# One decoder layer on one core: weight and activation tiles at other byte offsets in SBUF, and two of the three products of a K step in the other order

## The chip, the core and the metric

The kernel runs on one core of a Trainium2 chip. The metric is the device time of one execution in microseconds. The engines are named as in the profile: PE is TensorE's matmul, PEld its weight load, DVE is VectorE, ACT is ScalarE, POOL is GpSimd and SP is SyncE, whose queue issues most of the DMAs.

## The reference

One layer of a decoder in float32, for 256 tokens behind 16 meta tokens (T = 272), width 2048:

```python
q, c_kv, q_idx, k_idx, w_idx, u = split_columns(h @ w_in[l])
...
attn_out = jnp.einsum('bthc,chd->bthd', o_lat, w_uv[l]).reshape(B, T, ATTN_WIDTH)
pool_out = multiscale_pool(u, w_pool[l], pool_scale[l])
mix = jnp.concatenate([attn_out, pool_out], axis=-1) @ w_o[l]
h = layer_norm(ALPHA * h + mix, ln1_g[l], ln1_b[l])
f = conv_gated_ffn(h, w_up[l], conv_w[l], conv_b[l], w_down[l])
h = layer_norm(ALPHA * h + f, ln2_g[l], ln2_b[l])
```

`conv_gated_ffn` is a product of 2048 by 2 x 5632 columns, a causal convolution of width 3, a gated GELU and a product of 5632 by 2048. Almost all arithmetic is in four products: the input projection, `w_o`, `w_up` and `w_down`. The attention between them keeps the 64 best keys of each query.

## The kernel before

All weights come in tiles of 128 x 2048 float32, 1 MB each, in one fixed stream: 8 tiles of index queries, two small latent maps, 16 more projection tiles, 16 of `w_o`, then for the feed-forward part 88 tiles of `w_up` interleaved with the tiles of `w_down`. A tile is fetched by SP into `wraw`, and then split into an upper part, which ACT writes (L149, a copy rounded to the type that TensorE reads as fp32r), and a lower part, the remainder, which DVE writes (L150). Both go into one buffer `whl`; there are three of these and three of `wraw`. Activations are split in the same way into upper and lower parts, which lie together in one slot of a ring of 24.

`product` (L250 to L260) multiplies a weight tile with 16 activation slots, one K step of 128 for each. A K step is three matmuls into the same PSUM tile: upper weight x upper activation (L258), upper weight x lower activation (L259), lower weight x upper activation (L260). The weight block of 128 x 128 is the stationary operand, loaded by PEld for each matmul; the activation, 256 to 272 columns, streams. So one tile is 16 x 3 = 48 matmuls. The activations are named `xp` (the input, in the projection), `mixa` and `mixp` (attention and pooling, under `w_o`), `fold` (slots of another pool, for the first 8 tiles of `w_up`) and `hp` (the other 80 tiles of `w_up`). In `seven` (L855 to L857) and at L907 to L909 and L1061 to L1063, the products with `w_down`, the weights stream, 512 columns at a time, and a block of gated activations is stationary.

What matters here is where in a partition these operands begin, in bytes modulo 256. The pools are laid out by their sizes:

- A ring slot before has 2 x 272 floats, 2176 bytes, which is 8.5 times 256: neighbouring slots are 128 apart modulo 256. Inside a slot the class `Parts` puts the upper part of `mixa`, `mixp` and `hp` at 24 bytes and the lower part at 1120.
- A weight buffer before has 4160 floats, 65 times 256 bytes, so all three begin at the same place. The class `Split` puts the upper and the lower part of the first eight K steps at 0 and 4096 bytes, and those of the last eight at 8320 and 12416, which is 128 further modulo 256. The upper and the lower block of one K step are thus always at the same place. A `gap` tile of 64 bytes stands behind the buffers and shifts the ring by 64.
- The tables `K_PROJ`, `K_O` and `K_UP` say which K step stands at which place of a tile, so that slots of one kind meet the first half and slots of the other kind the second half.

Taken together, in the 80 tiles with `hp` the upper part of an activation always lies 216 bytes (modulo 256) behind the weight block that it meets, and the lower part 32 bytes behind it. Under `w_o` consecutive steps change between the two halves, since they are taken in another order (`order`).

The order of instructions on each engine comes from the program's order and a scheduler's rules; the PE queue runs in order.

Of the kernel before, what the change touches and what calls it, by code (L numbers as in the profile page):

```python
# [11 lines left out]
F32 = mybir.dt.float32  # L12
F32R = mybir.dt.float32r
# [4 lines left out]
P = 128  # L18
# [3 lines left out]
T = NM + S  # L22
Q0 = NM - 2
NQ = T - Q0
KT = D // P
# [42 lines left out]
class Split:  # L68

    def __init__(self, tile, sums):

        self.tile, self.places = tile, ((0, 1040), (2080, 3120)) if sums else ((0, 1024), (2080, 3104))

    def __getitem__(self, key):
        rows, part, c = key
        a, b = c.start, 2 * 1024 + 2 if c.stop is None else c.stop
        at = int(a >= 1024)
        assert b <= 1024 or at == 1  # L80
        o = self.places[at][part] - 1024 * at
        return self.tile[rows, o + a:o + b]


class Parts:


    def __init__(self, slot):
        flat = slot.rearrange("p a b -> p (a b)")
        self.parts = flat[:, 6:6 + NQ], flat[:, 280:280 + NQ]  # L90

    def __getitem__(self, key):
        return self.parts[key[1]][key[0], key[2]]

K_PROJ = (1, 3, 5, 7, 9, 11, 13, 15, 0, 2, 4, 6, 8, 10, 12, 14)
K_O = (1, 3, 5, 7, 9, 10, 12, 14, 0, 2, 4, 6, 8, 11, 13, 15)
K_UP = (1, 3, 5, 7, 8, 10, 12, 15, 0, 2, 4, 6, 9, 11, 13, 14)  # L100
# [3 lines left out]
def tile_layer(ctx, tc, xt, w_first, w_proj, w_uk, w_uv, w_pool, w_o, w_up, w_down, cols, rows, rel_bias, onehot, out):  # L104
    nc = tc.nc
    sb = ctx.enter_context(tc.tile_pool(name="sb", bufs=1))
    wp = ctx.enter_context(tc.tile_pool(name="wp", bufs=3))
    ring = ctx.enter_context(tc.tile_pool(name="ring", bufs=24))
# [12 lines left out]
    ps = small()  # L121
# [4 lines left out]
    stream = [w_proj[j] for j in range(8)] + [w_uk, w_uv] + [w_proj[j] for j in range(8, 24)]  # L126
    stream += [w_o[j] for j in range(KT)]
    plan = ffn_plan()
    kinds = {}
    for item in plan:  # L130
        if item[0] == "up":
            stream.append(w_up[item[2] * FT + item[1]])
        elif item[0] == "down":
            n = PARTS[FAST]
            stream.append(w_down[sum(PARTS[:FAST]) + n // 2 + (item[2] - 1) // 2 * (n // 4) + item[3]])
        else:
            kinds[len(stream)] = item[0]
            stream.append(w_down[sum(PARTS[:item[1]]) + item[2] * (PARTS[item[1]] // 2) + item[3]])
    stream += [w_down[d] for d in range(FT - PARTS[-1], FT)]
    spare, last = len(stream) - PARTS[-1], len(stream) - 1  # L140
# [29 lines left out]
            parts = split_part(raw, hl, slice(a, b))  # L170
        return parts

    def split_tile(sums=False):

        hl = Split(wp.tile([P, 4160], F32R, tag="whl", name="whl"), sums)
        if not state["use"]:

            wp.tile([P, 16], F32, tag="gap", name="gap", bufs=1)
        return hl

    def weight_tiles(sums=False):
        raw = wp.tile([P, 2048], F32, tag="wraw", name="wraw")
        return raw, split_tile(sums)

    def emit(i):
        if i in ready:
            return
        if i == last:

            raw = wp.tile([P, 2048], F32, tag="wraw", name="wraw")  # L190
            nc.sync.dma_start(raw, stream[i])
            raws[i] = raw
            ready[i] = []
            for c in range(0, 2048, 256):
                hl = ring.tile([P, 2, 258], F32R, tag="act", name="whl_r", padded_shape=[P, 2, T])
                nc.scalar.activation(hl[:, 0, :256], raw[:, c:c + 256], AF.Copy)
                nc.vector.tensor_tensor(hl[:, 1, :256], raw[:, c:c + 256], hl[:, 0, :256].bitcast(F32), op=ALU.subtract)
                ready[i].append(hl)
            return
        if i == spare:  # L200
            raw = wp.tile([P, 2048], F32, tag="wraw", name="wraw")
            hl = Split(sb.tile([P, 4160], F32R, tag="y", name="whl_y"), True)
        else:
            raw, hl = weight_tiles(i > spare)
        ready[i] = hl
        if i == VALUES:

            nc.sync.dma_start(raw, stream[i])
            held.extend((raw, hl))
            return  # L210
        split[i] = fetch(raw, hl, stream[i], kinds.get(i), i and i - 1 in split and split[i - 1][1])
        if i >= spare:
            raws[i] = raw
# [37 lines left out]
    def product(ps, hl, act, lo, hi, places, ks=None, k0=0, k1=KT):  # L251

        for n in range(k0, k1):
            k = (places if ks is None else ks)[n]
            w = slice(P * places.index(k), P * places.index(k) + P)
            wh, wl = hl[:, 0, w], hl[:, 1, w]
            ah, al = act[k][:, 0, lo:hi], act[k][:, 1, lo:hi]
            nc.tensor.matmul(ps, wh, ah, start=n == 0, stop=False)  # L258
            nc.tensor.matmul(ps, wh, al, start=False, stop=False)  # L259
            nc.tensor.matmul(ps, wl, ah, start=False, stop=n == KT - 1)  # L260

    at = ctx.enter_context(ExitStack())
    ap_ = at.enter_context(tc.tile_pool(name="attn", bufs=1))
# [3 lines left out]
    for k0, k1 in [(k, k + 1) for k in range(9)] + [(9, 12), (12, 15), (15, 16)]:  # L267
        if k0 == KT - 1:

            raw = ap_.tile([P, 1024], F32, name="wraw_l", tag="v1")[:, :T + MF].rearrange("p (a b) -> p a b", a=1)  # L270
        elif k0 % 3 == 0:
            raw = wp.tile([P, 2048], F32, tag="wraw", name="wraw")
            raw = raw[:, :3 * (T + MF)].rearrange("p (a b) -> p a b", b=T + MF)
        if k0 % 6 == 0:
            hl = split_tile()
        for w in ((slice(0, T), slice(T, T + MF)) if k0 == 0 else (slice(0, T + MF),)):
            nc.sync.dma_start(raw[:, k0 % 3:k0 % 3 + k1 - k0, w], w_first[k0:k1, :, w].rearrange("k p c -> p k c"))
        for k in range(k0, k1):
            xk, wk, a0 = raw[:, k % 3, :T], raw[:, k % 3, T:], k % 6 // 3 * 1024 + k % 3 * MF
            c = slice(a0, a0 + MF)  # L280
            a = ring.tile([P, 2, T], F32R, tag="act", name="xp")
            nc.scalar.activation(a[:, 0, :], xk, AF.Copy)
            nc.scalar.activation(hl[:, 0, c], wk, AF.Copy)
            nc.vector.tensor_tensor(a[:, 1, :], xk, a[:, 0, :].bitcast(F32), op=ALU.subtract)
            nc.vector.tensor_tensor(hl[:, 1, c], wk, hl[:, 0, c].bitcast(F32), op=ALU.subtract)
            x_parts.append(a)
            first.append((hl, c.start))
# [76 lines left out]
    ps = small()  # L364
# [225 lines left out]
    def values(h, pts, ptx):  # L590
        ps = small()
        hs = slice(h * HD, (h + 1) * HD)
        nc.tensor.matmul(ps[:, :NQ], vs[0][:, hs], ptx, start=True, stop=False)
        nc.tensor.matmul(ps[:, 2:NQ], vs[1][:, hs], pts[:, :2 * P], start=False, stop=False)
        nc.tensor.matmul(ps[:, 2 + P:NQ], vs[2][:, hs], pts[:, 2 * P:], start=False, stop=True)
        a = Parts(ring.tile([P, 2, T], F32R, tag="act", name="mixa"))
        nc.scalar.activation(a[:, 0, :NQ], ps[:, :NQ], AF.Copy)
        nc.vector.tensor_tensor(a[:, 1, :NQ], ps[:, :NQ], a[:, 0, :NQ].bitcast(F32), op=ALU.subtract)
        mix[h] = a
# [33 lines left out]
    def pooled(g, df, hl):  # L633
        for j in range(2):
            ps = small()
            for c in range(2):
                w = slice(256 * c + j * P, 256 * c + j * P + P)
                nc.tensor.matmul(ps[:, :NQ], hl[:, 0, w], df[:, c, 0, :], start=c == 0, stop=False)
                nc.tensor.matmul(ps[:, :NQ], hl[:, 0, w], df[:, c, 1, :], start=False, stop=False)
                nc.tensor.matmul(ps[:, :NQ], hl[:, 1, w], df[:, c, 0, :], start=False, stop=c == 1)  # L640
            m = 2 * g + j
            a = Parts(ring.tile([P, 2, T], F32R, tag="act", name="mixp"))
# [126 lines left out]
    def normalise(m):  # L769
        yd = y[:, m, Q0:]  # L770
        nc.vector.tensor_tensor(yd, yd, rs, op=ALU.mult)  # L771
        nc.vector.tensor_tensor(yd, yd, m2, op=ALU.add)
        nc.scalar.activation(yd, yd, AF.Identity, bias=col(LN1, 2 * m + 1), scale=col(LN1, 2 * m))
        a = Parts(ring.tile([P, 2, T], F32R, tag="act", name="hp"))
        nc.scalar.activation(a[:, 0, :NQ], yd, AF.Copy)
        nc.vector.tensor_tensor(a[:, 1, :NQ], yd, a[:, 0, :NQ].bitcast(F32), op=ALU.subtract)  # L776
        h_parts.append(a)
# [45 lines left out]
    def forms(r, j, whole):  # L823
# [9 lines left out]
        right = ring.tile([P, 2, T], F32R, tag="act", name="right")  # L833
# [321 lines left out]
```

## Time and profile before

| | |
|---|---|
| timed executions | 1034.94 us median of 2 (1034.75 to 1035.13) |
| span of the profiled execution | 1032.8 us, 2.1 us less than the median |
| PE busy | 1025.7 us, 7644 matmuls |
| PEld busy | 977.2 us, 7644 weight loads |
| DVE, ACT, POOL busy | 890.4, 622.4, 187.0 us |
| granted clock of TensorE | 0.997 of 2.4 GHz over the span |

The span runs from the first to the last instruction; what the timed executions have above it lies around the span. A PE row's duration overlaps the next matmul's, and its end is modelled. What a matmul costs in a stream is the time from its start to the start of the next, so the timeline's starts are what is read here, over as many matmuls as possible, since a start is printed to 0.01 us.

### The profile page before, as it was taken

What the parts mean: (1) busy time and instruction counts of PE and PEld (TensorE: products, weight loads), DVE (VectorE), ACT (ScalarE), POOL (GpSimd) and SP (SyncE); (2) the same over time, 40 slices, a digit from 0 to 9 for tenths busy, and PEclk for the clock granted to TensorE, in tenths of its full rate; (3) what the DMA queues carried; (4) which work ended last, traced back from release to release, by engine and by line L of the source; (5) the groups of instructions that cost most, each with busy time, mean ns of one, the idle gap of its engine ahead of it and who ended that gap; (6) DMA issues with size and microseconds to landing.
All of it is one profiled execution on the core that took longest, in us unless ns stands there. A gap on an engine that the chain in (4) does not pass through costs nothing.

```text
span 1032.8 us, 19199 instructions
## 1 busy us (share of the span) xinstructions
PE 1025.7 (99%) x7644; PEld 977.2 (95%) x7644; DVE 890.4 (86%) x1401; ACT 622.4 (60%) x1000; POOL 187.0 (18%) x245
## 2 busy tenths in 40 slices
PE   9999999999999999999999999999999999999997
PEld 8999999999999999999999999999999999999986
DVE  6878668758779998889999999999998999998976
ACT  7666446645448865655665555656556565565675
POOL 1200014125430022111121111211112111120031
PEclk9999999999999999999999999999999999999998
DMA  9755643454553569979887788877988878887875
GB/s 329 258 179 203 242 146 116 149 184 162 188 204 124 204 204 251 270 284 306 274 281 272 271 298 279 276 274 275 290 279 279 274 286 281 277 276 268 298 229 155
DMA packets 59754, 250.28 MB, mean 242 GB/s; under 512 B 21734, under 2 KB 22416, under 8 KB 32656
## 3 DMA queue, kind: packets, MB, share of 16 engines
q1 hardware_dynamic: 34592, 230.42, 61.7%
q0 software_dynamic: 7888, 16.14, 8.3%
q10 hardware_dynamic: 17184, 2.49, 1.5%
q8 instruction: 60, 0.98, 0.4%
q14 instruction: 30, 0.25, 0.1%
HBM read 232.50 MB, written 2.11 MB: 227 GB/s over the span
## 4 chain that ended last, share of the span: by engine, by line
PE 91%; DVE 4%; issue 2%; ACT 1%; POOL 1%; DMA 0%; SPq 0%; POOLq 0%; DVEq 0%; ACTq 0%
PE mm L260 22%; PE mm L258 22%; PE mm L259 22%; PE at L857 6%; PE at L856 6%; PE at L855 6%; PE mm L331 2%; DVE whl L150 1%; PE mm L909 1%; PE mm L908 1%; PE mm L907 1%; ACT whl L149 1%; DVE x L771 0%; DMA wraw<-in_w_first 0%; PE mm L559 0%
## 5 line engine op out<-in xcount | busy, mean ns | idle before, releaser
L150 DVE TENSOR_TENSOR whl<-wraw,whl 128x1024 fp32r<-128x1024 f32 (+1 forms) x416 | 486.8, 1205 | 35.7 <-ACT whl L149 34.7
L149 ACT ACTIVATE whl<-wraw 128x1024 fp32r<-128x1024 f32 (+1 forms) x416 | 403.1, 1015 | 108.1 <-DMA wraw<-in_w_up 21.4
L260 PE MATMUL mm<-hp,whl 128*128 128x258 f32 x1280 | 362.8, 283 | 0.0
L258 PE MATMUL mm<-hp,whl 128*128 128x258 f32 x1280 | 359.5, 281 | 0.0
L259 PE MATMUL mm<-hp,whl 128*128 128x258 f32 x1280 | 357.2, 279 | 0.3 <-DVE hp L776 0.3
L258 PEld LDWEIGHTS mm<-hp,whl 128*128 128x128 f32 x1280 | 243.8, 190 | 3.2
L259 PEld LDWEIGHTS mm<-hp,whl 128*128 128x128 f32 x1280 | 240.4, 188 | 3.7 <-DVE hp L776 0.5
L260 PEld LDWEIGHTS mm<-hp,whl 128*128 128x128 f32 x1280 | 240.2, 188 | 0.2
L258 PE MATMUL mm<-xp,whl 128*128 128x256 f32 (+5 forms) x384 | 111.3, 290 | 0.0
L260 PE MATMUL mm<-xp,whl 128*128 128x256 f32 (+5 forms) x384 | 108.6, 283 | 0.0
L259 PE MATMUL mm<-xp,whl 128*128 128x256 f32 (+5 forms) x384 | 108.5, 283 | 0.0
L790 ACT ACTIVATE z<-mm,cv 128x256 f32<-128x256 f32 x40 | 22.6, 566 | 91.1 <-PE mm L260 91.1
L827 POOL TENSOR_TENSOR forms<-za 128x128 f32<-128x128 f32 x20 | 21.9, 1093 | 306.2 <-DVE za L808 239.7
L258 PEld LDWEIGHTS mm<-xp,whl 128*128 128x128 f32 x384 | 72.3, 188 | 1.0 <-issue 0.5
L259 PEld LDWEIGHTS mm<-xp,whl 128*128 128x128 f32 x384 | 72.3, 188 | 0.4
L260 PEld LDWEIGHTS mm<-xp,whl 128*128 128x128 f32 x384 | 72.2, 188 | 0.0
L857 PE MATMUL at<-whl,gp 128*128 128x512 f32 x180 | 70.7, 394 | 0.0
L856 PE MATMUL at<-whl,gp 128*128 128x512 f32 x180 | 70.7, 394 | 0.0
L855 PE MATMUL at<-whl,gp 128*128 128x512 f32 x180 | 69.0, 393 | 0.0
L790 ACT ACTIVATE za<-mm,cv 128x256 f32<-128x256 f32 x40 | 22.7, 567 | 75.2 <-PE mm L260 66.9
L830 POOL TENSOR_TENSOR forms<-za 128x128 f32<-128x128 f32 x20 | 20.4, 1020 | 198.4 <-DVE za L808 184.5
L857 PEld LDWEIGHTS at<-whl,gp 128*128 128x128 f32 x180 | 33.8, 188 | 7.7
(349 smaller groups left out, 1888.1 us busy)
## 6 DMA issues: line engine op xcount, KB each, us to landing
wraw<-in_w_up SPq DMA_DIRECT2D x88, 1024.0 KB, 5.1
wraw<-in_w_down SPq DMA_DIRECT2D x80, 1024.0 KB, 6.6
wraw<-in_w_proj SPq DMA_DIRECT2D x24, 1024.0 KB, 5.1
wraw<-in_w_o SPq DMA_DIRECT2D x16, 1024.0 KB, 4.9
y<-v POOLq DMA_DIRECT2D x27, 256.0 KB, 8.2
y<-u POOLq DMA_DIRECT2D x18, 256.0 KB, 5.0
wraw<-in_w_first SPq DMA_DIRECT2D x8, 304.0 KB, 5.0
x<-in_xt SPq DMA_DIRECT2D x1, 2176.0 KB, 8.0
```

Source lines behind the costliest of these rows:

```text
L149: upper = nc.scalar.activation(hl[:, 0, c], raw[:, c], AF.Copy)
L150: lower = nc.vector.tensor_tensor(hl[:, 1, c], raw[:, c], hl[:, 0, c].bitcast(F32), op=ALU.subtract)
L258: nc.tensor.matmul(ps, wh, ah, start=n == 0, stop=False)
L259: nc.tensor.matmul(ps, wh, al, start=False, stop=False)
L260: nc.tensor.matmul(ps, wl, ah, start=False, stop=n == KT - 1)
L331: nc.tensor.matmul(ps[:m, :T], hl[:, t // 2, a0 + a:a0 + a + m], x_parts[k][:, t % 2, :], start=k == 0 and t == 0, stop=k == KT - 1 and t ...
L790: nc.scalar.activation(z, src[:, 2:NQ], AF.Identity, bias=col(C_B, j), scale=col(C_W, 3 * j + 2))
L827: nc.gpsimd.tensor_tensor(s[:, 0], a21, a22, op=ALU.add)
L830: nc.gpsimd.tensor_tensor(s[:, 3], a11, a21, op=ALU.subtract)
L855: nc.tensor.matmul(ps, a[:, 0, i], hl[:, 0, w], start=j == 0, stop=False)
L856: nc.tensor.matmul(ps, a[:, 0, i], hl[:, 1, w], start=False, stop=False)
L857: nc.tensor.matmul(ps, a[:, 1, i], hl[:, 0, w], start=False, stop=j == n - 1)
```

## The change

Four things change, and no arithmetic is added or removed.

1. A ring slot becomes 2 x 288 floats, 2304 bytes or 9 times 256, so that all slots begin at the same place modulo 256. The parts in a slot begin at 0 and 1088 bytes for K steps in the first half of `K_UP`, and at 8 and 1104 bytes for those in its second half (`ACTS`). `xp` keeps one tile of two rows, so its lower part now begins 1152 bytes behind the upper.
2. A weight tile number n has its upper part at 16 x (n mod 16) bytes and its lower part 8192 bytes plus 0, 48, 96, 144 or 208 further (`places`, `SHIFTS`), in one piece each. The buffer grows to 4352 floats (68 times 256 bytes). The tiles of `w_up` count from 72, so the 80 tiles with `hp` have the numbers 80 to 159 and go once through all 16 x 5 combinations. The `gap` tile goes.
3. In `product` the second and third matmul of a K step change places: the lower weight x upper activation now comes second.
4. The scratch for descriptors of POOL's DMAs is 8192 bytes per partition instead of 16384, which makes the room.

```diff
 class Split:
-    def __init__(self, tile, sums):
-        self.tile, self.places = tile, ((0, 1040), (2080, 3120)) if sums else ((0, 1024), (2080, 3104))
+    def __init__(self, tile, upper, lower):
+        self.tile, self.places = tile, (upper, lower)
...
 class Parts:
-    def __init__(self, slot):
+    def __init__(self, slot, k):
         flat = slot.rearrange("p a b -> p (a b)")
-        self.parts = flat[:, 6:6 + NQ], flat[:, 280:280 + NQ]
+        (a, b) = ACTS[k in K_UP[8:]]
+        self.parts = flat[:, a:a + NQ], flat[:, b:b + NQ]
...
+WIDE = 288
+ACTS = ((0, 272), (2, 276))
+SHIFTS = (0, 12, 24, 36, 52)
+
+def places(n):
+    upper = 4 * (n % 16)
+    return upper, upper + 2048 + SHIFTS[n // 16 % 5]
...
-        hl = Split(wp.tile([P, 4160], F32R, tag="whl", name="whl"), sums)
-        if not state["use"]:
-            wp.tile([P, 16], F32, tag="gap", name="gap", bufs=1)
-        return hl
+        return Split(wp.tile([P, 4352], F32R, tag="whl", name="whl"), *where)
...
-            raw, hl = weight_tiles(i > spare)
+            raw, hl = weight_tiles((0, 2112) if i > spare else places(order_of.get(i, i)))
...
             nc.tensor.matmul(ps, wh, ah, start=n == 0, stop=False)
-            nc.tensor.matmul(ps, wh, al, start=False, stop=False)
-            nc.tensor.matmul(ps, wl, ah, start=False, stop=n == KT - 1)
+            nc.tensor.matmul(ps, wl, ah, start=False, stop=False)
+            nc.tensor.matmul(ps, wh, al, start=False, stop=n == KT - 1)
...
-        a = Parts(ring.tile([P, 2, T], F32R, tag="act", name="hp"))
+        a = Parts(ring.tile([P, 2, WIDE], F32R, tag="act", name="hp"), m)
...
-    nc = _bacc.Bacc("TRN2", target_bir_lowering=False, num_devices=1)
+    nc = _bacc.Bacc("TRN2", target_bir_lowering=False, num_devices=1, dynamic_dma_scratch_size=8192)
```

On PE, two K steps of a tile of `w_up` in the middle of the feed-forward part (`mm` is the PSUM tile, `hp` with a number the slot, `whl` with a number the weight tile), before:

```order
L258 MATMUL mm_4886<-hp_3862,whl_4718 128x258
L259 MATMUL mm_4886<-hp_3862,whl_4718 128x258
L260 MATMUL mm_4886<-hp_3862,whl_4718 128x258
L258 MATMUL mm_4886<-hp_3874,whl_4718 128x258
L259 MATMUL mm_4886<-hp_3874,whl_4718 128x258
L260 MATMUL mm_4886<-hp_3874,whl_4718 128x258
```

and in the change:

```order
L263 MATMUL mm_4883<-hp_3859,whl_4715 128x258
L264 MATMUL mm_4883<-hp_3859,whl_4715 128x258
L265 MATMUL mm_4883<-hp_3859,whl_4715 128x258
L263 MATMUL mm_4883<-hp_3871,whl_4715 128x258
L264 MATMUL mm_4883<-hp_3871,whl_4715 128x258
L265 MATMUL mm_4883<-hp_3871,whl_4715 128x258
```

The slots, the tiles and the count of matmuls are the same; L264 is now the lower weight with the upper activation (L260 before), L265 the upper weight with the lower activation (L259 before). So the matmuls that share a weight block no longer follow each other, and those that share a streamed operand do.

On PE, where the first block of `seven` meets a tile of `w_up` (two accumulation groups in the same stretch), before:

```order
L857 MATMUL at<-whl,gp 128x512
L258 MATMUL mm<-hp,whl 128x258
L259 MATMUL mm<-hp,whl 128x258
L856 MATMUL at<-whl,gp 128x512
L857 MATMUL at<-whl,gp 128x512
L856 MATMUL at<-whl,gp 128x512
L857 MATMUL at<-whl,gp 128x512
L260 MATMUL mm<-hp,whl 128x258
```

and in the change:

```order
L862 MATMUL at<-whl,gp 128x512
L263 MATMUL mm<-hp,whl 128x258
L861 MATMUL at<-whl,gp 128x512
L862 MATMUL at<-whl,gp 128x512
L861 MATMUL at<-whl,gp 128x512
L862 MATMUL at<-whl,gp 128x512
L264 MATMUL mm<-hp,whl 128x258
L265 MATMUL mm<-hp,whl 128x258
```

One matmul of 258 columns stands four places later, behind the four of 512. One more like it, three places later, and two small matmuls that move by one or two places among the projection's are all that moved on PE beside the swap. On the other engines the order of the instructions is the same but for three neighbours on ACT and three on DVE that change places.

## Rows read from the trace of the kernel before

**Rows 1.** The page, parts 1 and 2: engines, and 40 slices.

```profile
PE 1025.7 (99%) x7644; PEld 977.2 (95%) x7644; DVE 890.4 (86%) x1401; ACT 622.4 (60%) x1000; POOL 187.0 (18%) x245
...
PE   9999999999999999999999999999999999999997
...
PEclk9999999999999999999999999999999999999998
```

**Rows 2.** Windows: stretch, length, then PE, PEld, DVE, ACT, POOL busy, PEclk, DMA.

```profile
400.00:500.00 100.00, 100.00 (x718) 94.15 (x717) 91.34 (x126) 60.67 (x86) 19.07 (x21) 1.00 0.87 281
...
800.00:900.00 100.00, 100.00 (x720) 94.21 (x719) 93.50 (x131) 60.95 (x87) 16.27 (x19) 1.00 0.82 277
```

**Rows 3.** The page, part 5: groups of instructions, count, busy us, mean ns.

```profile
L260 PE MATMUL mm<-hp,whl 128*128 128x258 f32 x1280 | 362.8, 283 | 0.0
L258 PE MATMUL mm<-hp,whl 128*128 128x258 f32 x1280 | 359.5, 281 | 0.0
L259 PE MATMUL mm<-hp,whl 128*128 128x258 f32 x1280 | 357.2, 279 | 0.3 <-DVE hp L776 0.3
```

**Rows 4.** Timeline of PE: start, duration; first matmuls of hp tiles 6 apart.

```profile
360.84 0.28 PE L258 MATMUL mm<-hp,whl 128*128 128x258 f32 x1
...
394.94 0.28 PE L258 MATMUL mm<-hp,whl 128*128 128x258 f32 x1
```

**Rows 5.** Timeline of PE: two single hp tiles, a block of `seven` between.

```profile
606.61 0.28 PE L258 MATMUL mm<-hp,whl 128*128 128x258 f32 x1
...
612.29 0.39 PE L855 MATMUL at<-whl,gp 128*128 128x512 f32 x1
...
615.07 0.28 PE L258 MATMUL mm<-hp,whl 128*128 128x258 f32 x1
...
631.28 0.28 PE L258 MATMUL mm<-hp,whl 128*128 128x258 f32 x1
...
637.05 0.39 PE L855 MATMUL at<-whl,right 128*128 128x512 f32 x1
```

**Rows 6.** Timeline of PE: `w_o`, first matmuls of tiles 9 apart.

```profile
249.44 0.28 PE L258 MATMUL mm<-mixp,whl 128*128 128x258 f32 x1
...
301.16 0.28 PE L258 MATMUL mm<-fold,whl 128*128 128x260 f32 x1
```

**Rows 7.** Timeline of PE: projection, first matmuls of tiles 6 apart.

```profile
98.15 0.28 PE L258 MATMUL mm<-xp,whl 128*128 128x258 f32 x1
...
132.59 0.28 PE L258 MATMUL mm<-xp,whl 128*128 128x258 f32 x1
```

**Rows 8.** Timeline of PE: folded tiles, first matmuls of tiles 7 apart.

```profile
308.77 0.28 PE L258 MATMUL mm<-fold,whl 128*128 128x260 f32 x1
...
348.90 0.28 PE L258 MATMUL mm<-hp,whl 128*128 128x258 f32 x1
```

**Rows 9.** Timeline of PE: four K steps of one hp tile.

```profile
600.07 0.28 PE L259 MATMUL mm<-hp,whl 128*128 128x258 f32 x1
600.18 0.28 PE L260 MATMUL mm<-hp,whl 128*128 128x258 f32 x1
...
600.42 0.28 PE L259 MATMUL mm<-hp,whl 128*128 128x258 f32 x1
600.54 0.28 PE L260 MATMUL mm<-hp,whl 128*128 128x258 f32 x1
```

**Rows 10.** Timeline of PE: projection, 12 matmuls of 266 columns.

```profile
163.64 0.29 PE L258 MATMUL mm<-xp,whl 128*128 128x266 f32 x1
...
165.14 0.41 PE L558 MATMUL mm<-kt,qt 128*128 128x144 f32 x2
```

**Rows 11.** Line L150: count, durations in ns least, median, most.

```profile
L150 DVE TENSOR_TENSOR whl<-wraw,whl x416: 682/1219/1671, 21.6 to 1003.2; 128x1024 fp32r<-128x1024 f32 x127, 128x512 fp32r<-128x512 f32 x12
```

**Rows 12.** Windows of line L150 alone: DVE busy.

```profile
800.00:900.00 100.00, 55.34 (x49) 1.00 0.82 277
```

**Rows 13.** The page, part 6: POOL's DMAs, count, KB, us to landing.

```profile
y<-v POOLq DMA_DIRECT2D x27, 256.0 KB, 8.2
```

More of the change, by code (lines that the diff above doesn't have):

```diff
@@ L68 @@
 class Split:
-    def __init__(self, tile, sums):
-        self.tile, self.places = tile, ((0, 1040), (2080, 3120)) if sums else ((0, 1024), (2080, 3104))
+    def __init__(self, tile, upper, lower):
+        self.tile, self.places = tile, (upper, lower)
     def __getitem__(self, key):
         rows, part, c = key
[L78 to L82, printed above, removed]
+        o = self.places[part]
+        return self.tile[rows, o + c.start:o + (2 * 1024 + 2 if c.stop is None else c.stop)]
 class Parts:
-    def __init__(self, slot):
+    def __init__(self, slot, k):
         flat = slot.rearrange("p a b -> p (a b)")
-        self.parts = flat[:, 6:6 + NQ], flat[:, 280:280 + NQ]
+        (a, b) = ACTS[k in K_UP[8:]]
+        self.parts = flat[:, a:a + NQ], flat[:, b:b + NQ]
     def __getitem__(self, key):
         return self.parts[key[1]][key[0], key[2]]
+WIDE = 288
[4 more added lines that the diff above has]
+    return upper, upper + 2048 + SHIFTS[n // 16 % 5]
 K_PROJ = (1, 3, 5, 7, 9, 11, 13, 15, 0, 2, 4, 6, 8, 10, 12, 14)
@@ L128, in tile_layer @@
     plan = ffn_plan()
-    kinds = {}
+    kinds, order_of, n_up = {}, {}, 0
     for item in plan:
         if item[0] == "up":
+            order_of[len(stream)] = n_up + 72
+            n_up += 1
             stream.append(w_up[item[2] * FT + item[1]])
@@ L171, in fetch, with split_tile, weight_tiles @@
         return parts
-    def split_tile(sums=False):
-        hl = Split(wp.tile([P, 4160], F32R, tag="whl", name="whl"), sums)
-        if not state["use"]:
-            wp.tile([P, 16], F32, tag="gap", name="gap", bufs=1)
-        return hl
-    def weight_tiles(sums=False):
+    def split_tile(where=(0, 2048)):
+        return Split(wp.tile([P, 4352], F32R, tag="whl", name="whl"), *where)
+    def weight_tiles(where):
         raw = wp.tile([P, 2048], F32, tag="wraw", name="wraw")
-        return raw, split_tile(sums)
+        return raw, split_tile(where)
     def emit(i):
@@ L194, in emit @@
             for c in range(0, 2048, 256):
-                hl = ring.tile([P, 2, 258], F32R, tag="act", name="whl_r", padded_shape=[P, 2, T])
+                hl = ring.tile([P, 2, 258], F32R, tag="act", name="whl_r", padded_shape=[P, 2, WIDE])
                 nc.scalar.activation(hl[:, 0, :256], raw[:, c:c + 256], AF.Copy)
@@ L201, in emit @@
             raw = wp.tile([P, 2048], F32, tag="wraw", name="wraw")
-            hl = Split(sb.tile([P, 4160], F32R, tag="y", name="whl_y"), True)
+            hl = Split(sb.tile([P, 4160], F32R, tag="y", name="whl_y"), 0, 2056)
         else:
-            raw, hl = weight_tiles(i > spare)
+            raw, hl = weight_tiles((0, 2112) if i > spare else places(order_of.get(i, i)))
         ready[i] = hl
@@ L280, in tile_layer @@
             c = slice(a0, a0 + MF)
-            a = ring.tile([P, 2, T], F32R, tag="act", name="xp")
+            a = ring.tile([P, 2, T], F32R, tag="act", name="xp", padded_shape=[P, 2, WIDE])
             nc.scalar.activation(a[:, 0, :], xk, AF.Copy)
@@ L595, in values @@
         nc.tensor.matmul(ps[:, 2 + P:NQ], vs[2][:, hs], pts[:, 2 * P:], start=False, stop=True)
-        a = Parts(ring.tile([P, 2, T], F32R, tag="act", name="mixa"))
+        a = Parts(ring.tile([P, 2, WIDE], F32R, tag="act", name="mixa"), h)
         nc.scalar.activation(a[:, 0, :NQ], ps[:, :NQ], AF.Copy)
@@ L641, in pooled @@
             m = 2 * g + j
-            a = Parts(ring.tile([P, 2, T], F32R, tag="act", name="mixp"))
+            a = Parts(ring.tile([P, 2, WIDE], F32R, tag="act", name="mixp"), 8 + m)
             nc.scalar.activation(a[:, 0, :NQ], ps[:, :NQ], AF.Copy, scale=col(G_POOL, m))
@@ L832, in forms @@
         mid = two_parts(slot(), s[:, :2])
-        right = ring.tile([P, 2, T], F32R, tag="act", name="right")
+        right = ring.tile([P, 2, T], F32R, tag="act", name="right", padded_shape=[P, 2, WIDE])
         right = two_parts(right[:, :, :2 * P].rearrange("p a (b c) -> p a b c", c=P), s[:, 2:])
```

## The prediction

> **What bounds the kernel.** The page comes first [rows 1]: PE is busy for 1025.7 of 1032.8 us, its slices are full from the second to the last but one, and its clock is granted in full, 0.997 of 2.4 GHz. The windows of the feed-forward part [rows 2] say the same by stage: PE 100.00 us of every 100, DVE 91 to 94, DMA at 0.82 to 0.87 of its engines. So nothing that makes DVE, ACT, POOL or a DMA a little faster or slower shows in the end, as long as it stays under PE, and anything that changes the pace of the matmuls shows in full. The question is thus the time from the start of one matmul to the start of the next.
>
> That pace is not set by the columns alone. At 2.4 GHz 258 columns take 107.5 ns. The reader should divide the tiles' times by their 48 matmuls. Six tiles with `hp` take 394.94 - 360.84 = 34.10 us, 5.683 us for one, 118.4 ns per matmul [rows 4]. The tiles under `w_o` stream the same 258 columns by the same three lines, and nine take 51.72 us: 5.747 each, 119.7 ns [rows 6]. Projection tiles of 258 columns take 34.44 / 6 = 5.740 us, 119.6 ns [rows 7]. The folded tiles take 40.13 / 7 = 5.733 us with 260 columns, 119.4 ns [rows 8], which by columns is 118.5 ns or 5.689 us at 258. Two tiles with `hp` differ too: 5.68 and 5.77 us [rows 5]. No wait lies between, and the granted clock is the same, so 0.06 us of a tile hangs on something else, and where the operands stand is what differs between these stages. Inside a K step it shows again: from L259 (lower activation) to L260 the starts are 0.11 and 0.12 us apart, in mean 0.115, while the other two intervals are near 0.12 [rows 9]; L259 is also the line with the shortest mean duration of the three [rows 3].
>
> **The change, part by part.** *Counts.* No matmul, load, copy or DMA is added or removed. L258 to L260 keep 1280 of each with `hp` [rows 3], that is 80 tiles, then 8 folded tiles, 16 under `w_o` and 24 in the projection.
>
> *The weights' places and the slots.* Before, the 80 tiles with `hp` all have the same two distances between stream and weights, 216 and 32 bytes. After, they go once through 80 combinations in steps of 16 bytes, and the lower weights have a distance of their own. So the new pace is a mean over places, and the trace of before has two samples of such a mean. (a) The folded tiles: their slots are 2080 bytes apart, 32 modulo 256, so that one tile goes through many distances. At 258 columns they give 5.689 us. (b) The tiles of the projection and of `w_o`, at distances or in orders of steps other than those of `hp`: 5.740 and 5.747 us.
>
> With (a) the 80 tiles change by 5.689 - 5.683 = +0.006 us each, +0.5 us in all; the 16 tiles under `w_o`, which would also come to 5.689, gain 16 x 0.058 = 0.9 us, and the 24 of the projection 24 x 0.051 = 1.2 us (the 16 that are not 258 columns wide taken as the others). The sum is -1.6 us. With (b) the 80 tiles cost 80 x 0.057 = +4.6 us and the rest stays. I see no reason to prefer one: (a) has the mixture, but in slots that change place with every step; (b) has places that stay for a whole tile, as they now do, but only a few of them. I take the middle, +1.5 us.
>
> *The swap.* The operands of the three matmuls and their number stay; only which load runs beside which stream changes. Before, the loads beside the streams (upper, lower, upper activation) were of (upper, lower, next upper) weights; now the streams are (upper, upper, lower) and the loads (lower, upper, next upper). The trace has no row of the new order. Its bounds come from the intervals inside a K step: at best every interval becomes 0.115 us [rows 9], at worst every matmul takes the slowest steady pace in the trace, 12 matmuls of 266 columns in 165.14 - 163.64 = 1.50 us, 125 ns, by columns 121.2 ns at 258 [rows 10]. Of the rows it is nearest to the mean over places, so the swap gets no term of its own: 0, with both ends kept for the range.
>
> *The 512-column products.* There the weights stream. Their stationary blocks lie in the pool of folded slots, so they already meet every distance: 12 matmuls take 615.07 - 612.29 = 2.78 us, 232 ns each [rows 5]. New places give another mixture of the same kind: 0. If each of the some 1000 of them moved by 1 ns it would be 1 us.
>
> *DVE and ACT* write and read the parts at other offsets. L150 takes 1219 ns in the median and is under PE's cover; DVE has 100 - 93.5 = 6.5 us of room in 100 [rows 2]. Cost 0; without the cover it is the last rival below.
>
> *The scratch of POOL's DMAs.* The accumulating DMAs land 8.2 us after issue [rows 13] and the next sum into the same columns of `y2` is a whole part of the feed-forward loop later, tens of microseconds. If less room for descriptors makes POOL wait, DVE's addition in the next part would be late only after that: 0. The three neighbours that change places on ACT and DVE are covered in the same way.
>
> The sum is 1032.8 + 1.5 = 1034.3 us of span; with the 2.1 us that the timed median has above the span, **1036.4 us, I say 1036.5**. 2% is 20.7 us, about what counts as a difference here, so the forecast is no change.
>
> **A rule that speaks against it.** The tiles of equal columns differ by 0.06 us though they run the same three lines [rows 4, 6]. The Trainium skill, in SBUF — State Buffer, section Who interferes with whom, says that PE's stream and its weight load have independent read ports and that PE never waits on anyone. By that rule a shift of places could not change the pace, and the time would stay 1034.9. The trace does not agree with it as it stands, since it leaves the 5.68 and the 5.77 us [rows 5] without a cause.
>
> **The rivals.**
>
> *Places do nothing* (0.12). The differences between stages would come from something else, their PSUM tiles or the order of their steps, and the new places leave every tile as it is: 1034.9 us. For it: I have no row in which the place alone differs. Against it: a tile's time is steady within a stage and differs between stages.
>
> *A faster K step* (0.15). The slots and weights now stand on multiples of 16 bytes for half of the K steps, and the same stream twice in a row may suit the swap. If two of the three intervals become the 0.115 us of L259, a K step takes 0.350 instead of 5.683 / 16 = 0.355 us: -0.005 x 1280 = -6.7 us with `hp`, and from 0.359 us under `w_o` and in the projection -0.009 x 16 x 40 = -5.8 us: 1022.4 us. Only if all three do, 0.345 us, does it pass 2%: -12.8, -9.0 and some -1 for the folded tiles, 1012 us. For it: such intervals exist. Against it: before, one interval in three has them, at one distance, and a mean over 16 places can't be all best ones. I give 0.03 of the 0.15 to passing 2%.
>
> *The places meet badly* (0.17), slower. The mechanism is the same, with the other sign: `hp`'s distances before are better than most, and the mean over the new ones is that of the slowest steady tile, 121.2 ns x 48 = 5.82 us. That costs 80 x 0.137 = 11.0 us, and 40 x 0.08 = 3.2 us in the other stages: 1049 us. It decides in the tiles of `w_up`: the time is over that of before as soon as their mean is over 5.69 us. For it: tiles under `w_o` and in the projection are all slower than `hp`'s. Against it: the folded tiles, which go through the most places, aren't.
>
> *DVE takes over* (0.03), slower by over 2%. DVE's copies of the lower part have 55.3 us in 100 [rows 12] and 6.5 us of room, so they decide once they take 12% longer, 1219 to some 1365 ns; some already take 1671 [rows 11]. At that length for all, 37% more, DVE would need 93.5 + 20.5 = 114 us where PE needs 100, over 600 us of feed-forward part: +84 us, some 1119. Against it: before, the buffers' parts lie at two places 128 bytes apart already, and the median over both is 1219 ns.
>
> **How the numbers follow.** The forecast has 0.53, places that do nothing 0.12 (the same to within 2 us), the faster K step 0.15, the bad places 0.17, DVE 0.03. The range has to hold 8 in 10: from 1029, halfway between the forecast and the faster K step, to 1043, halfway to the bad places. It leaves out about half of these two cases and the last, some 2 in 10. Faster by over 2%: the 0.03 with three short intervals. Slower by over 2%: DVE's 0.03. Within: 0.94.
>
> **What would show it.** In the profile of the changed kernel the 80 tiles with `hp` should no longer be 5.67 to 5.69 us with few at 5.77 but spread, from some 5.6 to 5.85, by their number modulo 16, in mean 5.69 to 5.74. The tiles of `w_o` and the projection should come down from 5.75 a little or stay. L150 should stay at 1219 ns, DVE at 91 to 94 in 100, and the blocks of 512 columns at 232 ns. The forecast is wrong if the tiles don't spread (places do nothing), if the mean leaves 5.62 to 5.80, or if a PE row shows a wait where none was.

## The result: 1042.5 us against 1034.9, and the profile after

The changed kernel takes 1042.53 us in the median of two executions (1042.49 and 1042.56), 1.0074 times the time before, with a 95% interval of [1.005, 1.0098] (intervals behind ratios are such below). That is slower by 7.6 us and within the 2% that counts as no difference. The forecast of 1036.5 was 6.0 us too low; the range of 1029 to 1043 just holds the time.

The page of the changed kernel, first its parts 1 and 2, as in [rows 1], then groups of part 5 for L263 to L265 (L258, L260 and L259 before, in this order), as in [rows 3]:

```profile
span 1040.7 us, 19199 instructions
...
PE 1033.0 (99%) x7644; PEld 983.8 (95%) x7644; DVE 890.9 (86%) x1401; ACT 620.6 (60%) x1000; POOL 185.5 (18%) x245
...
PEclk9999999999999999999999999999999999999998
...
L263 PE MATMUL mm<-hp,whl 128*128 128x258 f32 x1280 | 362.4, 283 | 0.0
L264 PE MATMUL mm<-hp,whl 128*128 128x258 f32 x1280 | 361.5, 282 | 0.0
L265 PE MATMUL mm<-hp,whl 128*128 128x258 f32 x1280 | 361.5, 282 | 0.0
```

The span is 7.9 us longer (1040.7 against 1032.8), with as many matmuls, the clock granted in full and no idle time ahead of these matmuls. So PE still sets the end and its matmuls take longer. The windows, which answer to [rows 2], show the other engines where they were:

```profile
400.00:500.00 100.00, 100.00 (x712) 94.19 (x712) 89.75 (x121) 59.86 (x85) 18.83 (x21) 1.00 0.84 277
800.00:900.00 100.00, 100.00 (x716) 94.36 (x714) 91.91 (x127) 60.92 (x88) 16.15 (x19) 1.00 0.84 282
```

PE is busy 100 us of 100, and does 712 and 716 matmuls in them where it did 718 and 720. The copies of the lower part, then at L150, have the duration of [rows 11] (least, median, most):

```profile
L159 DVE TENSOR_TENSOR whl<-wraw,whl x416: 677/1219/1668, 21.7 to 1011.4; 128x1024 fp32r<-128x1024 f32 x127, 128x512 fp32r<-128x512 f32 x12
```

The rest is in the timeline of PE, whose rows are start, duration and instruction. Here stand the first matmuls of the stages that [rows 4 to 8] show of before: six projection tiles, nine under `w_o`, seven folded tiles, six tiles with `hp`; then two single `hp` tiles (each up to the first 512-column matmul behind it), and the end of the last `hp` tile.

```profile
97.66 0.28 PE L263 MATMUL mm<-xp,whl 128*128 128x258 f32 x1
...
132.20 0.28 PE L263 MATMUL mm<-xp,whl 128*128 128x258 f32 x1
...
249.47 0.29 PE L263 MATMUL mm<-mixp,whl 128*128 128x258 f32 x1
...
301.40 0.29 PE L263 MATMUL mm<-fold,whl 128*128 128x260 f32 x1
...
309.00 0.28 PE L263 MATMUL mm<-fold,whl 128*128 128x260 f32 x1
...
349.32 0.28 PE L263 MATMUL mm<-hp,whl 128*128 128x258 f32 x1
...
361.04 0.28 PE L263 MATMUL mm<-hp,whl 128*128 128x258 f32 x1
...
395.61 0.28 PE L263 MATMUL mm<-hp,whl 128*128 128x258 f32 x1
...
847.21 0.28 PE L263 MATMUL mm<-hp,whl 128*128 128x258 f32 x1
...
852.89 0.39 PE L860 MATMUL at<-whl,right 128*128 128x512 f32 x1
...
920.59 0.28 PE L263 MATMUL mm<-hp,whl 128*128 128x258 f32 x1
...
926.42 0.40 PE L860 MATMUL at<-whl,gp 128*128 128x512 f32 x1
...
984.11 0.39 PE L860 MATMUL at<-whl,right 128*128 128x512 f32 x1
```

Per tile: the projection takes 34.54 / 6 = 5.757 us (5.740 before), `w_o` 51.93 / 9 = 5.770 (5.747), the folded tiles 40.32 / 7 = 5.760 (5.733), six tiles with `hp` 34.57 / 6 = 5.762 (5.683). Single tiles go from 5.68 to 5.83 us. Of before, the end of the last `hp` tile is this row:

```profile
977.00 0.39 PE L855 MATMUL at<-whl,right 128*128 128x512 f32 x1
```

So the stage with `hp`, its 512-column blocks included, took 977.00 - 348.90 = 628.10 us and takes 984.11 - 349.32 = 634.79: **+6.7 of the 7.9 us**. Up to its start 0.4 us were lost (349.32 against 348.90), behind it 0.8 us (56.6 against 55.8 us to the end of the span). Over 3838 of the 3840 matmuls with `hp` (all but two that wait), the mean from start to start went from 118.4 to 120.1 ns, which is 6.6 us.

What is lost behind the stage is of another kind. Three times PE halts there, at 1010.6, 1010.9 and 1018.2 us, for some 0.1, 0.1 and 0.5 us more than at the same instructions before; at the last halt the profile names the writer of a weight tile:

```profile
1018.76 0.39 PE L1067 MATMUL mm<-whl,gp 128*128 128x258 f32 x1 [0.28 <-DVE whl L254]
```

### The profile page after: what moved, and what is told of

It reads as the page before. It is cut to its first block, busy times and chain, and to the rows that moved or that the text cites. A ratio compares the mean times of both kernels' runs of the same rounds, so it can differ in the third digit from the quotient of the medians.

```text
span 1040.7 us, 19199 instructions
## 1 busy us (share of the span) xinstructions
PE 1033.0 (99%) x7644; PEld 983.8 (95%) x7644; DVE 890.9 (86%) x1401; ACT 620.6 (60%) x1000; POOL 185.5 (18%) x245
## 4 chain that ended last, share of the span: by engine, by line
PE 94%; issue 2%; DMA 1%; DVE 1%; POOL 1%; ACT 0%; SPq 0%; POOLq 0%; DVEq 0%; ACTq 0%
PE mm L263 24%; PE mm L265 24%; PE mm L264 24%; PE at L861 6%; PE at L860 6%; PE at L862 6%; PE mm L336 2%; DMA wraw<-in_w_down 1%; DVE whl L159 1%; POOL gb L979 0%; PE mm L564 0%; DMA wraw<-in_w_first 0%; PE at L599 0%; PE at L425 0%; PE at L426 0%
## 5 line engine op out<-in xcount | busy, mean ns | idle before, releaser
L263 PE MATMUL mm<-hp,whl 128*128 128x258 f32 x1280 | 362.4, 283 | 0.0
L264 PE MATMUL mm<-hp,whl 128*128 128x258 f32 x1280 | 361.5, 282 | 0.0
L265 PE MATMUL mm<-hp,whl 128*128 128x258 f32 x1280 | 361.5, 282 | 0.0
L264 PEld LDWEIGHTS mm<-hp,whl 128*128 128x128 f32 x1280 | 242.6, 190 | 3.1
L263 PEld LDWEIGHTS mm<-hp,whl 128*128 128x128 f32 x1280 | 242.1, 189 | 3.1
L265 PEld LDWEIGHTS mm<-hp,whl 128*128 128x128 f32 x1280 | 242.1, 189 | 0.4 <-DVE hp L781 0.2
L263 PE MATMUL mm<-xp,whl 128*128 128x256 f32 (+5 forms) x384 | 111.7, 291 | 0.0
L265 PE MATMUL mm<-xp,whl 128*128 128x256 f32 (+5 forms) x384 | 108.6, 283 | 0.0
L264 PE MATMUL mm<-xp,whl 128*128 128x256 f32 (+5 forms) x384 | 108.4, 282 | 0.0
L263 PEld LDWEIGHTS mm<-xp,whl 128*128 128x128 f32 x384 | 72.3, 188 | 0.6
L264 PEld LDWEIGHTS mm<-xp,whl 128*128 128x128 f32 x384 | 72.4, 188 | 0.4
L265 PEld LDWEIGHTS mm<-xp,whl 128*128 128x128 f32 x384 | 72.2, 188 | 0.5 <-issue 0.5
```

What stands on the lines that cost most here:

```text
L264: nc.tensor.matmul(ps, wl, ah, start=False, stop=False)
L265: nc.tensor.matmul(ps, wh, al, start=False, stop=n == KT - 1)
```

## The experiments

Below, a *cycle* is the three intervals of a K step as they repeat, in ns from start to start, in the order of the code: "116, 115, 116" is 115.6 ns in mean. *Places* are bytes within a weight buffer (upper, lower weights) and within a slot (upper, lower activation). The theory was that these places set the pace of a tile, and that the mean over 80 combinations is worse than the one before. The rivals were the swap, and the width of slots and buffers. Counts of tiles by their cycle are of the one profiled execution of a kernel, taken over the second half of each tile.

**The swap alone, and the change without it.** The first kernel is the one before with only this edit; the second is the changed kernel with it taken back.

```diff
-            nc.tensor.matmul(ps, wh, al, start=False, stop=False)
-            nc.tensor.matmul(ps, wl, ah, start=False, stop=n == KT - 1)
+            nc.tensor.matmul(ps, wl, ah, start=False, stop=False)
+            nc.tensor.matmul(ps, wh, al, start=False, stop=n == KT - 1)
```

> The kernel before with the second and third product of a K step swapped, all places as before. Theory 'places': what costs is that the distances between stream and weights are spread over all places; with both weight parts at one place and the old slots the distances stay 216 and 32 bytes, so hp stays near 118.4 ns per matmul and the time near 1035 us (1032 to 1038). Rival 'swap': the new order itself costs the 1.7 ns per matmul seen with hp, some 6.6 us: 1041 to 1042 us.

> The changed kernel with the old order of the three products, all new places kept. Theory 'places': still a mean over places, hp near 120.1 ns and 1042 us (1040 to 1044). Rival 'swap': back to 118.4 ns and 1035 us.

The swap alone took 1037.02 us, 1.0022 [1.0014, 1.0031]: `hp` 118.7 ns, `w_o` 120.4 where it was 119.7. The change without it took 1042.34 us, 1.0072 [1.006, 1.0084], with `hp` at 120.2 ns. So the swap costs some 2 us at the old places and nothing that shows at the new ones: it isn't the cause.

**One place for all tiles.** From the changed kernel:

```diff
-    upper = 4 * (n % 16)
-    return upper, upper + 2048 + SHIFTS[n // 16 % 5]
+    return 0, 2048
-ACTS = ((0, 272), (2, 276))
+ACTS = ((2, 276), (2, 276))
```

In the changed kernel the second half of the first `hp` tile, which stands at these places, had the cycle 116, 115, 116.

> The changed kernel with every weight tile at bytes 0 and 8192 and every slot of Parts at 8 and 1104 bytes: the one combination that in the changed kernel's first hp tile read 116, 115, 116 ns in its second half. Theory 'places': hp at 115.7 ns per matmul, 4.4 less than the changed kernel (-17 us), and the 16 tiles of w_o from 120.1 to the same (-3.4 us): some 1022 us, faster than both. If that half tile was short for another reason (its neighbours, the first tile of its kind), hp stays at 118 to 120 and the time at 1035 to 1042. Rival 'sizes' (the wider slots and buffers cost, not the place in them): 1042.

It took 1037.77 us, 1.0022 [1.0013, 1.0032], a miss by 16 us. Its timeline says why. Two first matmuls of tiles under `w_o`, nine tiles apart, and then two `hp` tiles at the same places:

```profile
243.37 0.28 PE L262 MATMUL mm<-mixp,whl 128*128 128x258 f32 x1
...
293.29 0.28 PE L262 MATMUL mm<-mixp,whl 128*128 128x258 f32 x1
...
587.83 0.28 PE L262 MATMUL mm<-hp,whl 128*128 128x258 f32 x1
...
593.69 0.40 PE L859 MATMUL at<-whl,gp 128*128 128x512 f32 x1
...
596.47 0.29 PE L262 MATMUL mm<-hp,whl 128*128 128x258 f32 x1
...
602.04 0.40 PE L859 MATMUL at<-whl,gp 128*128 128x512 f32 x1
```

Under `w_o` each of nine tiles takes 49.92 / 9 = 5.547 us, 115.6 ns. But of the 80 tiles with `hp` 41 settle into 127, 120, 120 (the first above, 5.86 us) and 37 into 116, 115, 116 (the second, 5.57 us). (The profiled execution took 1035.27 us, near the lower end of 1035.12 to 1039.75.) All 41 stand behind a block of 512 columns; the first nine tiles, which have none between them, are all of the other kind. So a place doesn't fix the pace; it fixes the few cycles that a tile can settle into. From here on a third theory stands beside the places and the widths: the entry, that is the state in which a tile begins, chooses the cycle.

**A slow place.** Upper weights at 128, lower at 8528, parts at 0 and 1088, which in the changed kernel gave 123, 122, 122:

```diff
+    return 32, 2132
+ACTS = ((0, 272), (0, 272))
```

> The changed kernel with all weight tiles at one of its slowest combinations: bytes 128 and 8528 (208 further), slots' parts at 0 and 1088; in the changed kernel a first half tile read 123, 122, 122 there. Theory 'places': hp at 122.3, w_o too, 1050 to 1054 us, the slowest of all with the same code. Rival 'history alone' (a place has no pace of its own, the entry decides): a mixture near 120, 1040 to 1044.

It took 1050.39 us, 1.0151 [1.0138, 1.0165], as expected, and the cycle is 122, 123, 122 under `w_o` and with `hp` alike. Six tiles with `hp` take 398.59 - 363.39 = 35.20 us, 5.867 each:

```profile
363.39 0.29 PE L262 MATMUL mm<-hp,whl 128*128 128x258 f32 x1
...
398.59 0.29 PE L262 MATMUL mm<-hp,whl 128*128 128x258 f32 x1
```

**The old distances in the new widths.** Four kernels with the old order of products and one place for all tiles, at which stream and weights are 216 and 32 bytes apart modulo 256, as before. They differ in where the whole set begins:

```diff
+    return 10, 2058   # ACTS ((0, 274), (0, 274)):   weights from 40
+    return 12, 2060   # ACTS ((2, 276), (2, 276)):   weights from 48
+    return 32, 2080   # ACTS ((22, 296), (22, 296)): weights from 128
+    return 16, 2064   # ACTS ((6, 280), (6, 280)):   weights from 64
```

> The changed kernel's wide slots and buffers and the old order of products, but one place for all: weights at 40 and 8232 bytes, slots' parts at 0 and 1096, so that the distances are again 216 and 32 bytes for every K step. Theory 'places': hp at 118.0 to 118.4 ns as before, w_o down from 119.7 to the same (-1.0 us): 1033 to 1035. Rival 'sizes': 1042.

> The changed kernel's wide slots and buffers, the old order of products, and for every K step weights at bytes 48 and 8240 and slots' parts at 8 and 1104: the distances 216 and 32 bytes again, and now also the old remainders modulo 16 (weights 0, upper activation 8, lower 0), which the last try with 40 bytes had not (weights 8, upper 0, lower 8). Theory 'places' (distance and the remainder modulo 16 decide which repeating cycle a tile settles into): hp settles at 118, 115, 120 as before, 118.4 ns with what the tile's first steps cost, w_o comes from 119.7 to 118: 1033 to 1036 us. Rival 'sizes' (the wider tiles or higher bits of the address decide): hp stays at 119.5 to 120, 1040 to 1042.

> Wide slots and buffers, old order of products, and every operand of hp and w_o at exactly the places modulo 256 that the second half of the tiles had before: weights at 224, upper activation at 184, lower at 0 (weights 128 bytes into the buffer, parts 88 and 1184 into the slot). Theory 'absolute place' (the places modulo 256 themselves, not only their distances, decide the cycle): all hp tiles settle at 118 or 120, 115, 120 ns, hp 118.0 to 118.4, w_o down from 119.7 to 118: 1032 to 1035 us. Rival 'sizes' (the wider slots or buffers, or higher bits of the address): hp at 119.4 to 120 as in the two tries before, 1038 to 1042.

> As the run beside it, all three operands 64 bytes back from there: weights at 160, upper activation at 120, lower at 192 modulo 256; distances 216 and 32 bytes and all remainders modulo 64 as before. If distance and the remainder modulo 64 decide: the same cycle, 118.0 to 118.4 ns and 1032 to 1035 us. If the place modulo 256 itself decides: another cycle, and a time between 1034 and 1042 that differs from the run beside it. Rival 'sizes': 1038 to 1042 for both.

From 40: 1041.69 us, 1.0063 [1.0051, 1.0075], all tiles with `hp` at 118, 122, 118. From 48: 1038.45, 1.0037 [1.0024, 1.0049], mostly 119, 117, 124. Both missed. From 128, which puts the operands of `hp` where those of a tile's second half lay before in SBUF modulo 256 (the first half was 128 further): 1035.57, 1.0002 [0.9993, 1.0011]. From 64, which is 64 bytes off that: 1033.81, 0.9986 [0.9977, 0.9995]. The last two have the same cycle, 119, 115, 120, in 70 and 71 of the 80 tiles, and 120, 121, 126 in nearly all others, the first ones; here is one tile of the first kernel, then the same tile of the second:

```profile
478.50 0.29 PE L262 MATMUL mm<-hp,whl 128*128 128x258 f32 x1
...
484.16 0.40 PE L859 MATMUL at<-whl,gp 128*128 128x512 f32 x1
```

```profile
477.80 0.28 PE L262 MATMUL mm<-hp,whl 128*128 128x258 f32 x1
...
483.45 0.39 PE L859 MATMUL at<-whl,gp 128*128 128x512 f32 x1
```

5.66 and 5.65 us. So the old places in the new widths give the old time back: neither the widths nor the scratch of POOL's DMAs nor the dropped `gap` cost anything that shows. A common shift by 64 leaves the cycle as it is, and the time to within 1.8 us, while shifts by 88 or 80 against the third kernel change it. Distances alone don't decide; distances with the remainder modulo 64 account for these four (with the remainder modulo 32 they would as well).

**The blocks ahead of the tiles.** If the entry chooses the cycle, other places of the gated activations, the stationary blocks of the 512-column products, should change the choice. From the kernel with one place, the gated slots grow to 2304 bytes, for which the weight buffers shrink to 4224 floats (first kernel; one line of several is shown), and their pool moves by 128 bytes as well (second):

```diff
...
-            a = fp.tile([P, 2, NE], F32R, name="gp", tag="gp", bufs=16)
+            a = fp.tile([P, 2, NE], F32R, name="gp", tag="gp", bufs=16, padded_shape=[P, 2, WIDE])
...
```

> The one place of the earlier run (weights 0 and 8192, parts 8 and 1104), and the 16 slots of the gated activations made 2304 bytes wide as the ring's, so that all blocks of 512 columns meet the same places (224 and 96 modulo 256); weight buffers 4224 floats to make the room. In the earlier run hp tiles settled into 116, 115, 116 ns or into 127, 120, 120 ns, 37 to 41, and which one went with the last matmuls of the block before. Theory 'entry' (the state in which the block before leaves PE picks the cycle): with all blocks alike, hp tiles come out nearly all in one of the two: 115.7 and some 1022 to 1026 us, or 122.2 and 1046 to 1050 us. Rival 'chance' (the cycle is picked by something else, such as DMA or DVE traffic): again a mixture, near 1037.

> As the kernel with even slots for the gated activations, with the pool of these slots moved by 128 bytes, so that they stand at 96 and 224 modulo 256, the same as the ring's. Theory 'entry': again nearly all hp tiles in one cycle, perhaps the other one: 1022 to 1026 or 1046 to 1050 us. Rival 'chance': near 1037, and the same mixture as with the other place.

1038.37 us, 1.0037 [1.0023, 1.0051], and 1040.22, 1.0052 [1.0039, 1.0064]. In the first, 46 tiles have 127, 120, 120 and the other 34 118, 118, 117 in some rotation; in the second 51 have 127, 120, 120, 20 have 116, 115, 116 and 9 the third. The mixture moves with places that no tile of `w_up` touches, as the entry theory has it; but not with one cycle for nearly all tiles, which was expected.

The blocks are in fact of two kinds: 12 matmuls with `gp` alone, or six with `right`, whose slots lie in the ring, and three with `gp`. Sorted by the kind ahead, the first kernel is nearly as the theory wants it: all 36 tiles behind `gp` alone have 127, 120, 120, and 33 of the 35 behind a block with `right` have 118, 118, 117. Here are one of either, between them a block with `right`:

```profile
496.06 0.39 PE L861 MATMUL at<-whl,gp 128*128 128x512 f32 x1
496.29 0.28 PE L262 MATMUL mm<-hp,whl 128*128 128x258 f32 x1
...
502.13 0.40 PE L859 MATMUL at<-whl,right 128*128 128x512 f32 x1
...
504.24 0.28 PE L262 MATMUL mm<-hp,whl 128*128 128x258 f32 x1
...
509.89 0.39 PE L859 MATMUL at<-whl,right 128*128 128x512 f32 x1
```

5.84 us behind `gp`, 5.65 behind `right`, at the same places. In the second kernel 35 of the 36 behind `gp` alone have 127, 120, 120, and those behind `right` are split, 19 at 116, 115, 116 and 16 at 127, 120, 120. In the kernel with one place, whose gated slots are 2080 bytes apart, both kinds are split.

**Two places, and one for each tile.** Again from the kernel with one place. The first kernel has 0 and 8192 for all tiles but the last 72 with `hp`; these have 240 and 8576. The second puts 13 of the 72 back, those that were at about 120 ns at 240 and at 115.6 in the kernel with one place.

```diff
+    return (60, 2144) if n >= 88 else (0, 2048)
...
+    return (60, 2144) if n >= 88 and n - 80 not in (8, 11, 19, 27, 35, 41, 47, 49, 55, 58, 61, 66, 69) else (0, 2048)
```

> An attempt at a faster kernel: new order of products, parts at 8 and 1104 bytes; weights at 0 and 8192 for w_o and the first 8 hp tiles, which settled at 116, 115, 116 ns in each earlier run at that place, and at 240 and 8576 for the 72 hp tiles behind blocks of 512 columns, where the changed kernel had a half tile at 118, 114, 115. Theory 'places', with a cycle that doesn't depend on the entry: hp at 115.7, 512-column blocks at 232: -9 us with hp and -3 us with w_o against before, 1021 to 1025 us. Theory 'entry': a mixture again in the 72 tiles, near 119, and 1033 to 1038 us.

> From e11_two_places, with 13 of the 72 tiles behind blocks back at weights 0 and 8192, places at which these 13 had the pace of 115.6 ns in e3_one_place, where e11 has them at about 120 ns. If a tile's pace follows from its own place and from the kind of block before it alone: the 13 tiles gain 13 x 48 x (120 - 115.6) ns = 2.7 us, the others keep theirs, some 1026.8 us and 116.5 ns in mean over the 80 tiles. If what went before a tile further back counts as well, its weight tiles among it: another mixture of the same paces, 1028 to 1032 us, with some of the 13 at 120 or 122 ns and some of the others moved.

The first took **1029.52 us, 0.9946 [0.9933, 0.9958]**, under both kernels: 45 of the 72 tiles have 118, 114, 115 and 27 some 120 ns, between what the two theories expected. The second took **1028.80 us, 0.9942 [0.9929, 0.9956]**, which the intervals don't tell from the first. Ten of its 13 tiles got 116, 115, 116 and three 118, 118, 117, and a few others left theirs. What is more, seven tiles changed that come ahead of all that was edited. Up to there the two kernels run the same instructions at the same places in the same order. The end of the first `hp` tile and the start of the second, in the first kernel, and that of the eighth:

```profile
353.65 0.28 PE L263 MATMUL mm<-hp,whl 128*128 128x258 f32 x1
354.03 0.39 PE L264 MATMUL mm<-hp,whl 128*128 128x258 f32 x1
354.25 0.28 PE L262 MATMUL mm<-hp,whl 128*128 128x258 f32 x1
...
387.54 0.28 PE L262 MATMUL mm<-hp,whl 128*128 128x258 f32 x1
```

and in the second:

```profile
351.98 0.28 PE L263 MATMUL mm<-hp,whl 128*128 128x258 f32 x1
352.31 0.39 PE L264 MATMUL mm<-hp,whl 128*128 128x258 f32 x1
352.54 0.28 PE L262 MATMUL mm<-hp,whl 128*128 128x258 f32 x1
...
386.46 0.28 PE L262 MATMUL mm<-hp,whl 128*128 128x258 f32 x1
```

PE halts here, so that L264 starts 0.38 us behind L263 in the one and 0.33 in the other. Behind it six tiles take 33.29 us in the one, 115.6 ns per matmul, and 33.92 in the other, 117.8 ns. Nothing in the program differs up to there, only the moments at which things happen. Three earlier kernels have the same places in these tiles and fit in: the one with one place halts 0.38 us at this matmul and takes 33.30 us for the six tiles, the second with wide gated slots 0.32 and 33.92, and the first of these doesn't halt there (0.12 us) and takes 35.18. That the halt is what chooses is likely by these five, but no run set it by itself. That the moments count fits what single executions show: the kernel with one place ran from 1035.12 to 1039.75 us, the one with gated slots of 2304 bytes from 1038.07 to 1042.27.

## Why the prediction was right, and where it was not

- *What bounds the kernel.* Right. PE stayed full and the time followed the matmuls' intervals; DVE's median copy stayed at 1219 ns and its share at 90 to 92 in 100.
- *The pace hangs on where the operands stand.* Shown: the same instructions take 115.6 ns at one set of places and 122.2 at another, 1050.4 us for the kernel at the slow one against 1028.8 for the best mixture. The rival that places do nothing is out. From the Trainium skill, SBUF — State Buffer, section Who interferes with whom, the prediction took a rule by which places can't change the pace. Read so, it is not borne out: the matmuls have no wait that the profile shows, but their pace changes with places alone. Whether the two reads that the page calls independent meet each other is not shown by these runs.
- *The size for the 80 tiles.* This is the term that failed. Between sample (a), +0.5 us, and sample (b), +4.6 us, the prediction took the middle with the rest of the stages and came to +1.5. Measured are +6.7 us in this stage, a mean of 120.1 ns or 5.766 us where 5.69 to 5.74 was said. Sample (b) alone would have missed by 2 us, and by luck: of its tiles, those under `w_o` stand at the same two distances as `hp` and only take the steps in another order, so they are no sample of other places. Sample (a) wasn't a mean over places that lasts: the folded tiles themselves went from 5.733 to 5.760 us, and the swap alone moves them by 0.6 ns a matmul. The range, made from the rivals' halfway points, held the time by 0.5 us; with this stage put at some +2.5 us and measured at +6.7, that was luck in good part.
- *The spread.* Said 5.6 to 5.85, found 5.68 to 5.83 over whole tiles (5.90 for the first, which waits). But not by the number modulo 16: the means for each upper place lie from 119.7 to 120.8 ns per matmul, those for each lower shift from 120.0 to 120.3, and single tiles from 117.7 to 121.7 (without waits and a tile's first intervals).
- *The other stages.* Nearly nothing, as in (b): +0.4 us up to the first `hp` tile, where (a) had -2.1. The 512-column products were costed at 0 with 1 ns as a bound; the mean of some 940 rose from 231.5 to 232.3 ns, and to 232.0 without two of the halts, which is 0.5 us, most of it among the 6.7. (Not all their stationary blocks lie with the folded slots, as the prediction had it: `right` lies in the ring.) The 0.8 us behind the stage are in the main the three halts there.
- *A wait where none was.* That was to show the forecast wrong, and there is one: the 0.28 us at L1067, behind the stage with `hp`. The prediction's cover for DVE didn't hold for this one tile. It is a small part of the 7.6 us, and why it arose was not tried.
- *The swap at 0.* Right at the new places (1042.34 without it, 1042.53 with it), not at the old places, where it is +2 us.
- *The rivals.* The time lies halfway between the forecast and "the places meet badly" (1049): that rival's sign and mechanism were right and its mean, 121.2 ns, was too high. The faster K step exists, but not in a mean: 115.6 ns at one place, in some executions.

What the prediction had no term for is that a place can have several cycles and that the way into a tile, as far as the runs go, chooses among them. The loss in the stage with `hp` comes from this: before, all tiles stood at one set of places (their two halves 128 bytes apart) whose mean is 118.4 ns; the change spreads them over 80 sets whose cycles average 120.1. That the places cause it is shown by the runs: without the swap the loss stays, and with the old places in the new widths it is gone. What inside the chip meets at these places, and why a shift by 64 doesn't count, stays open.

## What to carry to other kernels

When PE is full and the clock granted, divide a tile's start-to-start time by its matmuls and compare stages of the same shape: a difference of some ns without a wait was here a matter of where the operands begin and of how a tile is entered, and the best to the worst layout made 2% of the kernel. Spreading tiles over many places gives the mean, which is worse than one good place; look for a good one in the trace, and then time it, since a tile behind other work can settle into another cycle there: in one kernel here nearly all tiles went with the kind of block ahead, 5.65 or 5.84 us. For differences under 0.5% take several executions, because a program whose tiles have two cycles moves by 4 us on its own.

## What was not expected of the hardware

- Equal matmuls of 258 columns repeat with a period of one K step, with intervals of some 113 to 129 ns, in cycles such as 116, 115, 116, or 119, 115, 120, or 127, 120, 120.
- The Trainium skill, TensorE: Matmul & The Clock Gate, section Wait — 56ns, not 53.3ns?, gives columns over 2.4 GHz and some 2.5 ns from start to start of warm matmuls, which by estimate is 110 ns for 258 columns and, as it states, 215.7 for 512. No stage here shows that, with the clock at 0.997 of 2.4 GHz and a weight load for each matmul: 115.6 ns was the best steady cycle, and the products of 512 columns took 231.5 to 234.0 ns in mean.
- Shifting weights and streams together by 64 bytes keeps the cycle and nearly the time (1035.6 and 1033.8 us), by 80 or 88 it doesn't (1038.5 and 1041.7).
- The same code at the same places ran six tiles at 115.6 ns behind a halt of 0.38 us (two kernels), at 117.8 behind one of 0.32 or 0.33 (two), and at 122.1 without a halt there (one).
